# One more up projection by seven block products, and an even rate of wide pieces, in a two-layer decoder trunk

## The chip, the cores and the metric

The kernel runs on one core of a Trainium2 chip. The metric is the device time of one execution in microseconds (us); the time of the kernel before is the median of three runs.

## What is computed

Two post-norm residual layers on x, 256 tokens by 2048 channels, all in float32. Each layer has a mixer (layer 0: forgetting attention and block-sparse attention, layer 1: multi-head latent attention) and a SwiGLU feed-forward network. The change touches the feed-forward network alone:

```
for layer in range(DEPTH):                       # 2 layers
    y = mixer(x)
    x = layer_norm(alpha * x + y, ...)
    y = (silu(x @ w_gate) * (x @ w_up)) @ w_down  # 2048 -> 5632 -> 2048
    x = layer_norm(alpha * x + y, ...)
```

## The kernel before

**The work of TensorE** is a list of visits, written by `add_chunk` and `kmajor` and run in order by the loop at the end. A chunk is 512 output columns of one weight matrix; a visit takes 256 of its rows (a piece). float32 is had from three products of a high and a low part (`mm3`, lines 117 to 119): x high by w high, x high by w low, x low by w high.

**A plain piece** is 12 matmuls of 512 columns (two row blocks, two token tiles, three products). Its weights come by DMA into a `raw` tile, ScalarE copies them to the high part `wh` (line 425), VectorE subtracts to the low part `wl` (line 427).

**A wide piece** (`c.S`) does the same piece of a chunk by seven block products in place of eight (Winograd's form of Strassen's scheme): 21 matmuls of 256 columns into four PSUM banks A, B, C and D (`emit_s`, lines 453 to 455). Its weights need seven blocks, of which three are differences: VectorE makes these with three instructions (lines 383, 385, 386), ScalarE copies 1792 columns to `sh` (line 389), VectorE subtracts to `sl` (line 392). That last pair is owed and is paid behind the next piece's split (`owe`, `pay`). When a wide chunk is done, `drain_s` combines the four banks: one copy on ScalarE and five instructions on VectorE (lines 484 to 489). For an up chunk the product with the gate follows in one instruction (line 1093); a plain up has two (line 1089).

**The activations' blocks** for the wide pieces, `XS`, are made by `xs_batch` at the start of each feed-forward network, in four batches beside up 0 (VectorE lines 901 to 914).

**Order.** The network has 11 column groups f of 512. `ffn_part` first lists the plain visits: up f, and after f = 1, 3, 5, 7 and 10 the down projection of the groups so far (`down`). Gates 2 to 10 and the ups in `UPS` are wide; their pieces, in the order gate 2, gate 3, and so on, with an up of `UPS` right behind its gate, are mixed into the plain visits at a rate per plain visit k, `want`:

```
        for k, v in enumerate(flat):
            visits.append(v)
            want = max(want + (0 if k < 9 else 0.575 if k < 62 else 0.74 if k < 132 else 0.9),
                       ns + 1 if k in near else 0)
            while ns < min(len(gates), int(want)):
```

The product of gate and up is transposed on TensorE (`h_T`, line 602, four transposes a token tile) behind visits that `after_up` names: for a plain up, the first plain visit (f odd) or the second (f even) after its last piece; for a wide up, the first plain visit that begins a chunk. `ptile("tp")` puts the transposes into the pair of PSUM banks that the plain chunk before had, so they wait for VectorE twice: for the product (line 1089 or 1093) and for the reading of those banks (line 930 or 932 for a down chunk, which adds the result to the residual).

**Buffers.** Four pairs `wh`, `wl` serve plain pieces, two pairs `sh`, `sl` wide ones, while wide pieces are near; splits are made in the order of the pieces.

Of the kernel before, what the change touches and what calls it, by code (L numbers as in the profile page):

```python
# [53 lines left out]
def trunk_kernel(ctx: ExitStack, tc: tile.TileContext, x, ab_w_in, b_f, ab_w_out,  # L54
# [70 lines left out]
    def add_chunk(name, xs, kslots, srcs, tags=None):  # L125
        subs = []
        o = 0
        for n in srcs[0]:
            subs.append((n, o))
            o += n  # L130
        c = Chunk(name, xs, kslots, subs, srcs[1], tags or ("mm",) * len(subs))
        c.n = o
        chunks[name] = c
        return c

    def kmajor(c, hs=None):
        for h in (range(c.nh) if hs is None else hs):
            visits.append((c, h, (0, 1)))
# [18 lines left out]
    def lead_begin(c):  # L157
        for t in (0, 1):
            for h in range(LEAD):
                visits.append((c, h, (t,)))  # L160
        kmajor(c, range(LEAD, c.nh))

    def rows(w, k0, cols):
        return [(o, n, w[k0:k0 + 256, c0:c0 + n].rearrange("(k p) c -> p k c", p=P))
                for o, n, c0 in cols]
# [31 lines left out]

    GROUPS = ((0, 1), (2, 3), (4, 5), (6, 7), (8, 9, 10))
    NF = 11
    UPS = (4, 8)  # L200
    PLAIN = (0, 1)
    h_done = set()
    after_up = {}
# [2 lines left out]
    def ffn_part(layer):  # L206
        def wide(nm, w, f):
            return add_chunk(f"{nm}{layer}_{f}", "X", K16, ([512], lambda h: rows(
                w[layer], h * 256, [(0, 512, f * 512)])))

        def down(gi):
            grp = GROUPS[gi]
            slots = [4 * (f % 4) + k for f in grp for k in range(4)]
            for n in range(4):
                c = add_chunk(f"d{layer}_{gi}_{n}", "Y", slots, (
                    [512], lambda h, n=n: rows(
                        w_down[layer], grp[0] * 512 + h * 256, [(0, 512, n * 512)])))
                if gi == len(GROUPS) - 1 and n == 3:
                    (lead_final if layer == 1 else lead_end)(c)
                else:  # L220
                    kmajor(c)

        g0 = wide("g", w_gate, 0)
        g0.pair = 0
        lead_begin(g0)
        base = len(visits)
        for f in range(NF):
            if f == 1:
                kmajor(wide("g", w_gate, 1))
            c = wide("u", w_up, f)  # L230
            if f in UPS:
                c.S = True
            else:
                kmajor(c)
            if f in (1, 3, 5, 7):
                down(f // 2)
        down(len(GROUPS) - 1)
        flat = visits[base:]
        del visits[base:]
        ends = {}  # L240
        for f in range(NF):
            if f not in UPS:
                e = ends[f] = max(k for k, v in enumerate(flat) if v[0].name == f"u{layer}_{f}")
                o = e + 2 - f % 2
                after_up[layer, f] = [(v[0].name, v[1], v[2]) for v in flat[o:o + 3]]
        gates = []
        for f in range(len(PLAIN), NF):
            c = wide("g", w_gate, f)
            c.S = True
            gates += [(c, h, (0, 1)) for h in range(8)]  # L250
            if f in UPS:
                gates += [(chunks[f"u{layer}_{f}"], h, (0, 1)) for h in range(8)]
        near = {ends[f] + 2 for f in (1, 3, 5, 7, 9)}
        ns, want = 0, 0.0
        for k, v in enumerate(flat):
            visits.append(v)
            want = max(want + (0 if k < 9 else 0.575 if k < 62 else 0.74 if k < 132 else 0.9),
                       ns + 1 if k in near else 0)
            while ns < min(len(gates), int(want)):
                visits.append(gates[ns])  # L260
                ns += 1
                c = gates[ns - 1][0]
                f = int(c.name[3:])
                if ns % 8 == 0 and c.name[0] == "g" and f not in UPS:
                    assert k < ends[f] - 1, (k, ns, ends)
        assert ns == len(gates)
        for f in UPS:
            e = max(k for k, v in enumerate(visits) if v[0].name == f"u{layer}_{f}")
            rest = [v for v in visits[e + 1:] if not v[0].S]
            o = next(k for k, v in enumerate(rest) if v[1] == 0)  # L270
            after_up[layer, f] = [(v[0].name, v[1], v[2]) for v in rest[o:o + 2]]

    w_out_part("oa", ab_w_out[0])
    ffn_part(0)
    wi = mla_w_in[0]
    c = add_chunk("m0", "X", K16, ([512], lambda h: rows(wi, h * 256, [(0, 512, 0)])))
# [8 lines left out]
    for nm in order:  # L285
# [8 lines left out]
        kmajor(c)  # L294
    w_out_part("om", mla_w_out[0])
    ffn_part(1)


# [1163 lines left out]
```

## Time and profile before

| | |
|---|---|
| median of 3 runs (lowest, highest) | 2145.41 us (2145.27, 2146.47) |
| profiled execution, its own time | 2146.55 us |
| its span | 2144.7 us |
| granted TensorE clock, mean | 0.998 |
| TensorE / VectorE / ScalarE busy | 99% / 78% / 50% |
| HBM read | 402.56 MB, 190 GB/s over the span |

The span is that of the profiled execution; 1.9 us lie around it. Matmuls are pipelined and their ends are modelled, so a busy share of 99% does not show the gaps between matmuls; those are read from start times. The two feed-forward networks lie at about 436 to 1145 us and 1432 to 2144 us of the span.

### The profile page before, as it was taken

To read this page: it belongs to the slowest core of one execution; us is meant where nothing else is said; L and a number is where in the kernel's file an instruction comes from. 1 tells how busy PE (TensorE), PEld (TensorE's weight loads), DVE (VectorE), ACT (ScalarE), POOL (GpSimd) and SP (SyncE) were. 2 spreads that over 40 slices of the span, in tenths; PEclk is the share of its full clock that TensorE was granted. 3 is DMA by queue.
4 is the path that set the end of the run, shared out by engine and by line. 5 is a ranking of instruction groups with operands and counts; after the bars stand their busy time and mean duration, and the time that the engine had idled before them with its cause. 6 is when DMAs were issued, how large, how long until landed. Compare 5 with 4: busy or idle time off the path is not lost.

```text
span 2144.7 us, 31708 instructions
## 1 busy us (share of the span) xinstructions
PE 2120.4 (99%) x12570; PEld 1864.7 (87%) x12570; DVE 1674.0 (78%) x2173; ACT 1061.6 (50%) x1212; POOL 94.5 (4%) x142
## 2 busy tenths in 40 slices
PE   9999999999999999999999999999999999999998
PEld 9899998788888888888888999878888888888886
DVE  5555656798888998899866676688888989889875
ACT  5444544355545555555534665445444555555551
POOL 2100000100000000000001331010000000000000
PEclk9999999999999999999999999999999999999999
DMA  8565555556555556555865533745555556555582
GB/s 287 176 204 165 172 184 199 198 174 207 195 191 190 189 190 203 187 187 184 295 193 164 176 129 137 284 139 182 188 189 192 180 190 203 187 190 199 184 293 77
DMA packets 230341, 410.41 MB, mean 191 GB/s; under 512 B 14089, under 2 KB 58161, under 8 KB 229169
## 3 DMA queue, kind: packets, MB, share of 16 engines
q1 hardware_dynamic: 230192, 408.40, 57.3%
q8 instruction: 98, 1.61, 0.3%
q14 instruction: 51, 0.41, 0.1%
HBM read 402.56 MB, written 5.78 MB: 190 GB/s over the span
## 4 chain that ended last, share of the span: by engine, by line
PE 58%; issue 35%; DVE 5%; ACT 1%; POOL 1%; DMA 0%; SPq 0%; DVEq 0%; ACTq 0%; POOLq 0%
PE mm L117 11%; PE mm L118 11%; PE mm L119 11%; PE mm L512 3%; PE mm L516 3%; PE mm L514 3%; PE tp L602 2%; PE att L118 1%; PE att L119 1%; PE att L117 1%; PE sA L454 1%; PE sB L454 1%; PE sC L454 1%; PE sC L455 1%; PE sB L453 1%
## 5 line engine op out<-in xcount | busy, mean ns | idle before, releaser
L425 ACT ACTIVATE wh<-raw 128x1024 fp32r<-128x1024 f32 (+3 forms) x403 | 417.5, 1040 | 416.2 <-PE mm L119 161.9
L427 DVE TENSOR_TENSOR wl<-raw,wh 128x1024 fp32r<-128x1024 f32 (+3 forms) x403 | 482.3, 1206 | 133.1 <-ACT wh L425 131.9
L392 DVE TENSOR_TENSOR sl<-sraw,sh 128x1792 fp32r<-128x1792 f32 x176 | 356.2, 2024 | 64.6 <-ACT sh L389 63.9
L389 ACT ACTIVATE sh<-sraw 128x1792 fp32r<-128x1792 f32 x176 | 298.9, 1698 | 145.1 <-DVE sraw L386 141.9
L117 PE MATMUL mm<-wh,XH 128*128 128x512 f32 (+3 forms) x820 | 319.9, 390 | 0.0
L118 PE MATMUL mm<-wl,XH 128*128 128x512 f32 (+3 forms) x820 | 316.8, 386 | 0.0
L119 PE MATMUL mm<-wh,XL 128*128 128x512 f32 (+3 forms) x820 | 316.3, 386 | 0.0
L117 PE MATMUL mm<-wh,YH 128*128 128x512 f32 (+1 forms) x768 | 303.9, 396 | 0.0
L118 PE MATMUL mm<-wl,YH 128*128 128x512 f32 (+1 forms) x768 | 302.9, 394 | 0.0
L119 PE MATMUL mm<-wh,YL 128*128 128x512 f32 (+1 forms) x768 | 302.4, 394 | 0.0
L119 PEld LDWEIGHTS mm<-wh,XL 128*128 128x128 f32 x820 | 153.9, 188 | 33.2
L117 PEld LDWEIGHTS mm<-wh,XH 128*128 128x128 f32 x820 | 154.4, 188 | 28.0
L118 PEld LDWEIGHTS mm<-wl,XH 128*128 128x128 f32 x820 | 154.1, 188 | 27.7
L119 PEld LDWEIGHTS mm<-wh,YL 128*128 128x128 f32 x768 | 144.1, 188 | 34.6
L117 PEld LDWEIGHTS mm<-wh,YH 128*128 128x128 f32 x768 | 144.5, 188 | 29.6
L118 PEld LDWEIGHTS mm<-wl,YH 128*128 128x128 f32 x768 | 144.2, 188 | 29.5
L383 DVE TENSOR_TENSOR sraw<-sraw 128x512 f32<-128x512 f32 x176 | 120.5, 685 | 0.0
L512 PE MATMUL mm<-XH,wh 128*128 128x256 f32 x364 | 104.3, 286 | 0.0
L514 PE MATMUL mm<-XH,wl 128*128 128x256 f32 x364 | 102.6, 282 | 0.0
L516 PE MATMUL mm<-XL,wh 128*128 128x256 f32 x364 | 102.5, 282 | 0.0
L453 PE MATMUL sA<-sh,XH 128*128 128x256 f32 x352 | 100.9, 287 | 0.0
L454 PE MATMUL sA<-sl,XH 128*128 128x256 f32 x352 | 98.8, 281 | 0.5 <-DVE sl L392 0.4
(302 smaller groups left out, 4447.6 us busy)
## 6 DMA issues: line engine op xcount, KB each, us to landing
raw<-in_ffn_w_down_dram SPq DMA_DIRECT2D x160, 512.0 KB, 5.2
sraw<-in_ffn_w_gate_dram SPq DMA_DIRECT2D x149, 512.0 KB, 3.9
raw<-in_ffn_w_up_dram SPq DMA_DIRECT2D x137, 512.0 KB, 4.7
raw<-in_ab_w_in_dram SPq DMA_DIRECT2D x80, 256.0 KB, 3.1
sraw<-in_ffn_w_up_dram SPq DMA_DIRECT2D x39, 512.0 KB, 3.9
raw<-in_ffn_w_gate_dram SPq DMA_DIRECT2D x27, 512.0 KB, 4.6
sraw<-in_ab_w_in_dram SPq DMA_DIRECT2D x48, 256.0 KB, 3.3
raw<-in_ab_w_out_dram SPq DMA_DIRECT2D x22, 512.0 KB, 3.6
```

The source lines that it names most:

```text
L117: nc.tensor.matmul(o, lh, rh, start=start, stop=False)
L118: nc.tensor.matmul(o, lh, rl, start=False, stop=False)
L119: nc.tensor.matmul(o, ll, rh, start=False, stop=stop)
L389: nc.scalar.activation(sh, r[:, 256:2048], AF.Copy)
L392: nc.vector.tensor_tensor(sl, r[:, 256:2048], sh.bitcast(F32), op=ALU.subtract)
L425: nc.scalar.activation(wh[:, a:b], r[:, a:b], AF.Copy)
L427: nc.vector.tensor_tensor(wl[:, a:b], r[:, a:b], wh[:, a:b].bitcast(F32), op=ALU.subtract)
L453: nc.tensor.matmul(o, h, w[0][:, q], start=first, stop=False)
L454: nc.tensor.matmul(o, h, w[1][:, q], start=False, stop=False)
L512: nc.tensor.matmul(o, wh[:, kk, a:a + P], XH[:, slot, :], start=first, stop=False)
L514: nc.tensor.matmul(o, wl[:, kk, a:a + P], XH[:, slot, :], start=False, stop=False)
L516: nc.tensor.matmul(o, wh[:, kk, a:a + P], XL[:, slot, :], start=False, stop=last)
```

## The change

`UPS` becomes (2, 4, 8): the eight pieces of up 2 are wide in both layers, where they were plain. The rate is 0 for the first seven plain visits and 0.77 per plain visit after them, in place of 0 for nine, 0.575 to visit 61, 0.74 to visit 131 and 0.9 from there.

```diff
-    UPS = (4, 8)
+    UPS = (2, 4, 8)
...
-            want = max(want + (0 if k < 9 else 0.575 if k < 62 else 0.74 if k < 132 else 0.9),
+            want = max(want + (0 if k < 7 else 0.77),
                        ns + 1 if k in near else 0)
```

Layer 0's list had 173 plain and 88 wide visits behind gate 0, and has 165 and 96 now (layer 1's has seven more plain visits, at its very end). The wide ones ended behind plain visit 138, and end behind 130; the plain visits after that are as many as before. The order moves on all engines; three places on VectorE matter below. In the rows, `raw` and `sraw` are loaded weights, `wl`, `sl` low parts, `xt` and `gt` the tiles of up and of gate, `X` the residual.

**Up 0's end, layer 0.** Before, from the split of the piece ahead of gate 2's first:

```order
L427 TENSOR_TENSOR wl_95<-raw_91,wh_94 128x1024
L914 TENSOR_TENSOR XS_4150<-gt_3530,XS_4149 128x1024
L383 TENSOR_TENSOR sraw_93<-sraw_93 128x512
L385 TENSOR_TENSOR sraw_93<-sraw_93 128x256
L386 TENSOR_TENSOR sraw_93<-sraw_93 128x256
L1089 TENSOR_TENSOR gt_3529<-gt_3529,mm_4131 128x512
L1089 TENSOR_TENSOR gt_3529<-gt_3529,mm_4132 128x512
L427 TENSOR_TENSOR wl_97<-raw_88,wh_96 128x1024
L392 TENSOR_TENSOR sl_103<-sraw_93,sh_102 128x1792
```

Now, from the blocks of gate 2's second piece:

```order
L383 TENSOR_TENSOR sraw_93<-sraw_93 128x512
L385 TENSOR_TENSOR sraw_93<-sraw_93 128x256
L386 TENSOR_TENSOR sraw_93<-sraw_93 128x256
L901 TENSOR_TENSOR xt_3526<-XH,XL 128x1024
L392 TENSOR_TENSOR sl_103<-sraw_93,sh_102 128x1792
L906 TENSOR_TENSOR gt_3530<-xt_3526 128x2x128
L907 TENSOR_TENSOR gt_3530<-gt_3530,xt_3526 128x2x128
L908 TENSOR_TENSOR gt_3530<-xt_3526 128x2x128
L909 TENSOR_TENSOR gt_3530<-xt_3526,gt_3530 128x2x128
L427 TENSOR_TENSOR wl_97<-raw_88,wh_96 128x1024
L914 TENSOR_TENSOR XS_4146<-gt_3530,XS_4145 128x1024
L1089 TENSOR_TENSOR gt_3529<-gt_3529,mm_4127 128x512
```

Between the first batch of `XS` and up 0's product (line 1089), layer 0 had the blocks of one wide piece and no `sl`; now it has the blocks and the `sl` of two. Layer 1 had the blocks and the `sl` of one and three whole batches; now it has two of each and the fourth batch's line 914 too. On TensorE the first wide piece now stands ahead of the plain visit behind which up 0 is transposed.

**Up 4's end, layer 0.** Before, with the reading of the last down chunk's banks (line 932) first:

```order
L932 TENSOR_TENSOR X_3525<-X_3525,mm_5982 128x512
L932 TENSOR_TENSOR X_3525<-X_3525,mm_5983 128x512
L392 TENSOR_TENSOR sl_103<-sraw_93,sh_102 128x1792
L484 TENSOR_TENSOR xt_3526<-xt_3526,sD_5721 128x256
L485 TENSOR_TENSOR xt_3526<-xt_3526,sA_5720 128x256
L486 TENSOR_TENSOR xt_3526<-xt_3526,sB_5722 128x2x256
L488 TENSOR_TENSOR xt_3526<-xt_3526,sB_5722 128x256
L489 TENSOR_TENSOR xt_3526<-xt_3526,sC_5723 128x2x256
L1093 TENSOR_TENSOR gt_3529<-gt_3529,xt_3526 128x1024
```

Now:

```order
L484 TENSOR_TENSOR xt_3526<-xt_3526,sD_5913 128x256
L485 TENSOR_TENSOR xt_3526<-xt_3526,sA_5912 128x256
L486 TENSOR_TENSOR xt_3526<-xt_3526,sB_5914 128x2x256
L488 TENSOR_TENSOR xt_3526<-xt_3526,sB_5914 128x256
L489 TENSOR_TENSOR xt_3526<-xt_3526,sC_5915 128x2x256
L1093 TENSOR_TENSOR gt_3529<-gt_3529,xt_3526 128x1024
L383 TENSOR_TENSOR sraw_93<-sraw_93 128x512
L385 TENSOR_TENSOR sraw_93<-sraw_93 128x256
L386 TENSOR_TENSOR sraw_93<-sraw_93 128x256
L427 TENSOR_TENSOR wl_97<-raw_88,wh_96 128x1024
L932 TENSOR_TENSOR X_3525<-X_3525,mm_6146 128x512
L932 TENSOR_TENSOR X_3525<-X_3525,mm_6147 128x512
```

The reading of the banks moved from ahead of the drain to behind it and behind a split. On TensorE, one plain visit stood between up 4's last piece and its transposes, and two stand there now. Up 8 had three plain visits and a wide one there, and has two plain ones now, in the same order as up 4.

**Up 2's end, layer 0, now** (it was plain before):

```order
L930 SCALAR_TENSOR_TENSOR X_3525<-X_3525,mm_4918 128x512
L930 SCALAR_TENSOR_TENSOR X_3525<-X_3525,mm_4919 128x512
L392 TENSOR_TENSOR sl_105<-sraw_92,sh_104 128x1792
L484 TENSOR_TENSOR xt_3526<-xt_3526,sD_4703 128x256
L485 TENSOR_TENSOR xt_3526<-xt_3526,sA_4702 128x256
L486 TENSOR_TENSOR xt_3526<-xt_3526,sB_4704 128x2x256
L488 TENSOR_TENSOR xt_3526<-xt_3526,sB_4704 128x256
L489 TENSOR_TENSOR xt_3526<-xt_3526,sC_4705 128x2x256
L1093 TENSOR_TENSOR gt_3529<-gt_3529,xt_3526 128x1024
```

This is the order that up 4 had before, with one plain visit between the last piece and the transposes.

## Rows read from the trace of the kernel before

**Rows 1.** The page, its span and its part 1.

```profile
span 2144.7 us, 31708 instructions
...
PE 2120.4 (99%) x12570; PEld 1864.7 (87%) x12570; DVE 1674.0 (78%) x2173; ACT 1061.6 (50%) x1212; POOL 94.5 (4%) x142
```

**Rows 2.** Timeline of TensorE: start us, us, engine, line, operation [idle before].

```profile
1008.87 0.28 PE L453 MATMUL sA<-sh,XH 128*128 128x256 f32 x1
...
1011.36 0.39 PE L117 MATMUL mm<-wh,XH 128*128 128x512 f32 x1
...
1014.14 0.40 PE L117 MATMUL mm<-wh,XH 128*128 128x512 f32 x1
```

**Rows 3.** Busy time by stretch, layer 0: PE, PEld, DVE, ACT, POOL, clock, DMA.

```profile
467.00:691.00 224.00, 223.30 (x1285) 194.41 (x1284) 190.96 (x217) 113.57 (x99) 0.00 (x0) 1.00 0.58 195
691.00:1016.00 325.00, 323.21 (x1936) 284.65 (x1935) 294.65 (x343) 167.17 (x141) 0.00 (x0) 1.00 0.57 190
```

**Rows 4.** Waits of VectorE, 467 to 691 us: total us, times, longest.

```profile
DVE wl L427 <- ACT wh L425: 16.4, 17, 1.8
DVE sl L392 <- ACT sh L389: 11.5, 25, 1.0
```

**Rows 5.** Waits of VectorE, 691 to 1016 us.

```profile
DVE sl L392 <- ACT sh L389: 18.2, 31, 0.9
DVE wl L427 <- ACT wh L425: 3.0, 6, 0.6
```

**Rows 6.** Timeline of TensorE, layer 0: the first transposes after ups 0, 1, 4, 8.

```profile
463.88 0.60 PE L602 MATMUL tp<-ident,gt 128*128 128x128 f32 x4
...
527.41 0.66 PE L602 MATMUL tp<-ident,gt 128*128 128x128 f32 x4 [0.70 <-DVE gt L1089]
...
701.18 0.40 PE L119 MATMUL mm<-wh,YL 128*128 128x512 f32 x1
702.93 0.66 PE L602 MATMUL tp<-ident,gt 128*128 128x128 f32 x4 [1.35 <-DVE gt L1093]
...
965.30 0.66 PE L602 MATMUL tp<-ident,gt 128*128 128x128 f32 x4 [0.22 <-DVE X L932]
```

**Rows 7.** The same, layer 1: ups 0, 1, 4, 8.

```profile
1460.19 0.65 PE L602 MATMUL tp<-ident,gt 128*128 128x128 f32 x4 [0.50 <-DVE gt L1089]
...
1524.35 0.65 PE L602 MATMUL tp<-ident,gt 128*128 128x128 f32 x4 [1.30 <-DVE gt L1089]
...
1699.86 0.66 PE L602 MATMUL tp<-ident,gt 128*128 128x128 f32 x4 [1.34 <-DVE gt L1093]
...
1962.84 0.66 PE L602 MATMUL tp<-ident,gt 128*128 128x128 f32 x4 [0.81 <-DVE X L932]
```

**Rows 8.** Timeline of VectorE: up 0's products, layer 0 and layer 1.

```profile
463.01 1.28 DVE L1089 TENSOR_TENSOR gt<-gt,mm 128x512 f32<-128x512 f32 x2
...
1458.86 1.28 DVE L1089 TENSOR_TENSOR gt<-gt,mm 128x512 f32<-128x512 f32 x2
```

**Rows 9.** Timeline of VectorE, layer 0, around up 4's end.

```profile
698.89 0.42 DVE L484 TENSOR_TENSOR xt<-xt,sD 128x256 f32<-128x256 f32 x1
...
701.65 1.22 DVE L1093 TENSOR_TENSOR gt<-gt,xt 128x1024 f32<-128x1024 f32 x1
702.79 0.68 DVE L383 TENSOR_TENSOR sraw<-sraw 128x512 f32<-128x512 f32 x1
...
704.31 1.22 DVE L427 TENSOR_TENSOR wl<-raw,wh 128x1024 fp32r<-128x1024 f32 x1
705.44 0.68 DVE L114 TENSOR_TENSOR YL<-tp,YH 128x512 fp32r<-128x512 f32 x1
```

**Rows 10.** Timeline of VectorE, layer 0, around up 8's end.

```profile
953.28 2.03 DVE L392 TENSOR_TENSOR sl<-sraw,sh 128x1792 fp32r<-128x1792 f32 x1 [0.77 <-ACT sh L389]
955.22 0.41 DVE L484 TENSOR_TENSOR xt<-xt,sD 128x256 f32<-128x256 f32 x1
...
964.57 1.28 DVE L932 TENSOR_TENSOR X<-X,mm 128x512 f32<-128x512 f32 x2
```

## The prediction, made before the change was run

> **What bounds the kernel.** I read the page first: TensorE is busy for 99% of the span, VectorE for 78% [rows 1]. The first figure hides small gaps, since ends are modelled; so I took start times next. A wide piece takes 1011.36 - 1008.87 = 2.49 us on TensorE, a plain one 14.14 - 11.36 = 2.78 us [rows 2]. The list of visits, at these prices, is what sets the time: the order leaves TensorE few waits. Then the busy time by stretch, for whoever might be late: at a rate of 0.575 wide pieces VectorE is busy 191.0 of 224 us (85%), at 0.74 it is 294.7 of 325 us (91%), with TensorE at its full clock of 2.4 GHz in both [rows 3]. What the rest of VectorE's time is, its waits say. A wait of `wl` for ScalarE's `wh` mostly means that VectorE is ahead and has no free buffer: 16.4 us at 0.575 [rows 4], only 3.0 us at 0.74 [rows 5]. The wait of `sl` for `sh` (18.2 us in 31 waits there) is the latency of the wide split itself and gives nothing back. So at 0.74 VectorE's chain fills some 99% of the time (3.0 of 325 us are left); at 0.575 it had 7% to spare. Last, the transposes of the product, where TensorE waits for VectorE by name [rows 6, 7]. The bracket counts from a modelled end: from 701.18 to 702.93 is 1.75 us where 0.23 is usual, so 1.52 us are lost against a bracket of 1.35. I add 0.17 to each bracket: 0.87, 1.52 and 0.39 us in layer 0 (ups 1, 4, 8), 0.67, 1.47, 1.51 and 0.98 us in layer 1 (ups 0, 1, 4, 8), 7.4 us in all.
>
> **The change, term by term.** A difference of 0.2%, 4.3 us, is about what a measurement of this kernel can tell from none.
>
> *The products.* 16 pieces (8 in each layer) go from 2.78 to 2.49 us: -16 x 0.29 = **-4.6 us**. All of it lies on TensorE's path, since TensorE has work at every moment there. Bytes and DMA issues stay the same, a wide piece is the same 512 KB; SP's and POOL's queues get nothing new.
>
> A rule of the Trainium skill speaks against this term. The page "TensorE: Matmul & The Clock Gate", section "Back-to-back issue gap", says that in a stream of weight loads and matmuls both set the spacing, about 81 ns at 128 columns and 131 ns at 512; halfway, as an estimate, 98 ns at 256 columns, so that 21 short matmuls would cost 2.06 us against 1.57 us for 12 long ones and the term would be +7.8 us. The trace disagrees: 2.49 / 21 = 119 ns against 2.78 / 12 = 232 ns [rows 2].
>
> *VectorE's work.* The price of a wide split is its blocks, 704.31 - 702.79 = 1.52 us [rows 9], and its `sl`, 955.22 - 953.28 = 1.94 us [rows 10]; a plain split is 705.44 - 704.31 = 1.13 us [rows 9]. Where VectorE is ahead, this is covered. I go through the places where TensorE waits for it.
>
> *Up 0.* The first wide piece comes two plain visits earlier, into the stretch in which VectorE makes `XS`. In layer 0 the product's first half ended at 463.01 + 0.68 = 463.69 [rows 8], 0.2 us ahead of the transposes at 463.88, which did not wait [rows 6]. By the order, VectorE now has 1.52 + 2 x 1.94 = 5.4 us more ahead of that product, and TensorE one wide piece, 2.49 us: a stall of up to 5.4 - 2.5 - 0.2 = 2.7 us. Short waits that VectorE has there can take part of it; none to all, I take 2.0. In layer 1 it gets 1.52 + 1.94 + 1.13 (line 914, priced as the split of the same size) = 4.6 us more; 4.6 - 2.5 + 0.67 = 2.8, I take 2.4, which is 1.7 over the old stall. Together **+3.7 us** (0 to 4.8).
>
> *Up 1.* Its transposes stood one plain visit behind its last piece; now a wide visit of 2.49 us comes between, more than either stall. The 0.87 and 1.47 us go: **-2.3 us** (0 if VectorE is late by as much).
>
> *Up 2.* It was plain and had no stall. Now it has the order that up 4 had, with one plain visit (2.78 us) to hide the drain and the product, which took from 698.89 to 702.87 [rows 9]. That cost 1.52 us at up 4, so **+3.0 us** in two layers (2 to 5).
>
> *Ups 4 and 8.* Both now have two plain visits, 5.56 us, but the banks for the transposes are read by line 932 behind the drain. From the end of the up's last piece: before, at up 4 this was 701.18 + 0.23 - 2.78 = 698.63, and the drain began 0.26 later. Drain and product take 702.79 - 698.89 = 3.90 us, the next blocks 1.52, a plain split 1.13, the first half of line 932 0.68: 7.5 us, a stall of 1.9 us. At up 8 the drain began 1.14 us behind that end (955.22 against 964.91 less three plain visits and a wide one), because `sl` waited for `sh` [rows 10]; with that it is 2.8 us. In layer 1 the transposes wait for the second half, 0.6 us more, as the stalls of up 8 show (0.39 and 0.98). I take 2.3 and 2.9 us: 10.4 us for four, less the 4.4 us they cost before: **+6.0 us** (4.4 to 9).
>
> *The rest.* Transposes of plain ups 3, 5, 7 and 9 keep a wide visit ahead of them and had no stall. The tail behind the wide pieces has the same plain visits as before. ScalarE, half idle, does 8 longer copies a layer and is waited for only through VectorE; I cost it at nothing.
>
> Sum: -4.6 + 3.7 - 2.3 + 3.0 + 6.0 = +5.8 us, so 2152.3 from the profiled execution's 2146.55 us. Its own time lies 1.1 us above the median of the runs; from that, 2151.2 us.
>
> A check from VectorE's side. A layer adds 8 x (1.52 + 1.94) = 27.7 us of wide splits, 8 x 0.35 = 2.8 us of waits for `sh` (18.2 us [rows 5] over the 52 wide pieces that 325 us hold at 0.74), 3.90 - 1.28 = 2.6 us for up 2's drain and product in place of its two plain products, and drops 8 x 1.13 = 9.0 us: 24 us. It had 16.4 + 3.0 = 19.4 us in which it was ahead [rows 4, 5]. If all of that can be used it falls behind by 4.7 us a layer, +9 us in all. So **VectorE becomes the bound of the stretch**, and the two ways of counting agree within 4 us. The stalls above are counted at their places, so I keep to them and add 0.8 us for short waits for `sl`: **2152.0 us**.
>
> **The rivals.**
>
> *VectorE keeps ahead (faster).* If short waits inside VectorE's order close up and the order at ups 0, 2, 4 and 8 costs no more than before, what is left is -4.6 - 2.3: 2138.5 us. For it: the early stretch did have 16 us to spare. Against: line 1089 was only 0.2 us early in layer 0. It decides at whether VectorE begins the products within 0.3 us of their due time.
>
> *Ups 4 and 8 stay as they were (same).* If the banks are read in time, +6.0 goes: 2146.0 us with the small waits. For it: at up 8 line 932 stood behind the drain before too, and only 0.39 and 0.98 us were lost. Against: a plain visit and a wide one less stand there now to hide it.
>
> *VectorE's lead can't be used (slower by more).* If only three quarters of the 19.4 us are worth anything, it falls behind by 24 - 14.6 = 9 us a layer: 2163 us. For it: an even rate leaves it no stretch to recover in.
>
> *Weight loads set the spacing (slower).* Loads were busy for 1864.7 us in 12,570, 148 ns each [rows 1]; 21 of them would be 3.1 us, over a plain piece's 2.78: +5.3 in place of -4.6 us, 2162 us with the stalls. Against: rows 2 show 119 ns a matmul. This is the place of the skill's rule above, which the rows don't bear out.
>
> **How the numbers follow.** Forecast 0.50 (its own range 2147 to 2158), VectorE ahead 0.14, ups 4 and 8 as before 0.22, lead unusable 0.12, loads 0.02. Faster by over 0.2% (under 2141.1) is the first rival, 0.14. Same (to 2149.7) is the second, 0.22, and a quarter of the forecast, 0.12. Slower is the rest, 0.52. The range from 2143 to 2162 leaves out the first rival and a third of the case with the lead unusable (its own range is 2157 to 2169), and takes in the loads' 2162 us: 0.18.
>
> **What would show it.** In the changed profile: wide pieces still 2.49 us; transposes with a bracket of 1 to 3 us behind ups 0, 2, 4 and 8 in both layers, none behind up 1; those of ups 4 and 8 released by line 932; VectorE at 90% or more from 470 us on, with its waits for `wh` down to a few us a layer. I am wrong if ups 4 and 8 wait under 1 us, if the waits for `wh` stay above 10 us a layer, or if TensorE's longest waits stand at wide pieces, for `sl`, and not at transposes.

## The result and the profile after

The changed kernel takes **2176.05 us** (median of 4 runs, 2175.20 to 2178.81), the kernel before 2145.94 us beside it (4 runs, 2145.27 to 2146.80): a ratio of 1.0142, 95% interval 1.0125 to 1.0160. It is slower by 30 us. The forecast was 2152.0 us, with a range from 2143 to 2162: the sign was right, the size was not, and the range missed.

The page of the changed kernel, its span and its part 1 [rows 1 are those of before]; the profiled execution took 2178.81 us itself:

```profile
span 2176.7 us, 32083 instructions
PE 2128.8 (98%) x12714; PEld 1876.7 (86%) x12714; DVE 1712.9 (79%) x2229; ACT 1076.9 (49%) x1214; POOL 94.5 (4%) x142
```

The page hides the loss almost wholly: TensorE is busy 98% in place of 99%, and part of the 8.4 us that it gained in busy time is matmuls that ran slower. So I read the transposes by the timeline, as [rows 6, 7] were read. TensorE, the first transposes after ups 0, 2, 4 and 8 in layer 0, then the same in layer 1:

```profile
469.27 0.84 PE L602 MATMUL tp<-ident,gt 128*128 128x128 f32 x4 [2.69 <-DVE gt L1089]
...
564.98 0.65 PE L602 MATMUL tp<-ident,gt 128*128 128x128 f32 x4 [1.35 <-DVE gt L1093]
...
722.02 1.00 PE L602 MATMUL tp<-ident,gt 128*128 128x128 f32 x4 [3.65 <-DVE X L932]
...
976.04 0.66 PE L602 MATMUL tp<-ident,gt 128*128 128x128 f32 x4 [1.43 <-DVE X L932]
...
1478.71 0.66 PE L602 MATMUL tp<-ident,gt 128*128 128x128 f32 x4 [2.47 <-DVE gt L1089]
...
1575.72 1.12 PE L602 MATMUL tp<-ident,gt 128*128 128x128 f32 x4 [2.68 <-DVE gt L1093]
...
1736.71 1.12 PE L602 MATMUL tp<-ident,gt 128*128 128x128 f32 x4 [4.96 <-DVE X L932]
...
1992.19 0.66 PE L602 MATMUL tp<-ident,gt 128*128 128x128 f32 x4 [1.58 <-DVE X L932]
```

Each stands where the prediction put it, with the releaser it named, and up 1 has none. With 0.17 added to each bracket they make 22.2 us; 17.8 were forecast and 7.4 were there before. That is +14.8 us of the span's +32.0 (2176.7 less 2144.7).

**A term that the sum did not have** shows in the granted clock. Busy time by stretch of the changed kernel (columns as in [rows 3]; the clock is third from the end), behind up 0's transposes and behind up 4's:

```profile
469.60:473.00 3.40, 3.40 (x18) 3.40 (x17) 3.33 (x6) 1.50 (x1) 0.00 (x0) 0.50 0.00 0
473.00:476.40 3.40, 3.40 (x20) 2.91 (x20) 3.40 (x4) 1.64 (x3) 0.00 (x0) 1.00 0.02 5
...
722.20:725.60 3.40, 3.40 (x18) 3.40 (x18) 3.40 (x4) 2.49 (x3) 0.00 (x0) 0.50 0.02 3
```

For 3.4 us TensorE ran at 1.2 GHz in place of 2.4. There are five such stretches in the two networks, at 469.6, 722.2, 1479.9, 1575.5 and 1735.9 us (the last of 6.8 us). Each goes with one of the five brackets of 2.47 us or more: the last two begin 0.2 and 0.8 us before the wait ends, the others behind it; the three brackets of 1.35 to 1.58 us had none behind them. The networks of the kernel before had none but at the very end. TensorE's timeline in the longest, the first matmuls of one wide piece and of the plain piece after it:

```profile
1737.48 0.56 PE L453 MATMUL sA<-sh,XH 128*128 128x256 f32 x1
...
1742.11 0.63 PE L117 MATMUL mm<-wh,YH 128*128 128x512 f32 x1
```

The piece took 4.63 us, 2.49 is usual [rows 2]. By start times the five stretches cost 1.7, 1.8, 1.6, 1.7 and 3.0 us, **9.8 us** in all.

**A second one** is a group of waits at the third piece of a down chunk. Some come from ScalarE's queue, which I had costed at nothing. ScalarE's timeline, changed kernel, at the end of up 3 (columns as before, ACT is ScalarE):

```profile
662.06 0.38 ACT L483 ACTIVATE gt<-sA 128x256 f32<-128x256 f32 x1
667.28 1.06 ACT L1084 ACTIVATE gt<-gt 128x1024 f32<-128x1024 f32 x1 [4.83 <-DVE gt L489]
668.25 1.04 ACT L425 ACTIVATE wh<-raw 128x1024 fp32r<-128x1024 f32 x1
669.19 0.58 ACT L113 ACTIVATE YH<-tp 128x512 fp32r<-128x512 f32 x1
```

The Silu of a wide gate (line 1084) waits for the end of the drain on VectorE, and behind it, in the same queue, waits the copy of the transposed product to `YH`, which the down chunk needs. TensorE's timeline there:

```profile
669.82 0.51 PE L117 MATMUL mm<-wh,YH 128*128 128x512 f32 x1 [0.85 <-ACT YH L113]
...
671.20 0.50 PE L119 MATMUL mm<-wh,YL 128*128 128x512 f32 x1 [0.64 <-DVE YL L114]
```

By start times the waits at this place lost 6.7 us at ups 3 and 7 of both layers, and none before. Only 2.0 us of them are waits for ScalarE's `YH`, at up 3. Another 1.6 us are for `YL` (line 114) at up 3, just behind, and 3.0 us are for `YL` at up 7, where no Silu stands in the way. Up 7 in layer 0, VectorE and TensorE:

```profile
945.27 0.68 DVE L114 TENSOR_TENSOR YL<-tp,YH 128x512 fp32r<-128x512 f32 x1
```

```profile
946.01 0.51 PE L119 MATMUL mm<-wh,YL 128*128 128x512 f32 x1 [1.41 <-DVE YL L114]
```

VectorE came to line 114 without a wait of its own, straight from two plain splits and an `sl`, while `YH` had been done since 943.4 us: that is VectorE's lateness again. Waits of wide pieces for `sl` grew by another 3.5 us or so. With the products' -4.6: -4.6 + 14.8 + 9.8 + 6.7 + 3.5 = 30.2 of the 32.0 us.

**Why VectorE is late** I read from its own chain, from the first batch of `XS` (line 901) to the last `sl` (line 392). Before, this runs in layer 0 from 438.8 to 1050.5 us and in layer 1 from 1434.5 to 2047.5; after, from 435.5 to 1065.3 and from 1445.2 to 2081.4. Busy time in these stretches, first before, then after (DVE is the third figure behind the comma, without the counts):

```profile
438.80:1050.50 611.70, 609.18 (x3556) 532.33 (x3555) 544.10 (x632) 314.73 (x269) 0.00 (x0) 1.00 0.57 192
1434.50:2047.50 613.00, 608.81 (x3554) 532.03 (x3553) 544.28 (x632) 314.57 (x269) 0.00 (x0) 1.00 0.57 192
```

```profile
435.50:1065.30 629.80, 616.46 (x3649) 541.24 (x3648) 566.22 (x663) 324.79 (x274) 0.00 (x0) 0.99 0.57 190
1445.20:2081.40 636.20, 619.69 (x3649) 543.50 (x3648) 566.96 (x663) 324.70 (x274) 0.00 (x0) 0.99 0.56 188
```

And VectorE's waits in layer 0's stretch, before and after:

```profile
DVE sl L392 <- ACT sh L389: 31.9, 59, 1.0
DVE wl L427 <- ACT wh L425: 19.4, 23, 1.8
```

```profile
DVE sl L392 <- ACT sh L389: 45.4, 67, 3.0
DVE wl L427 <- ACT wh L425: 8.0, 13, 1.6
```

The chain grew by 18.1 us in layer 0 and 23.2 in layer 1. VectorE's idle time in it, the length less the busy time, was 67.6 and 68.7 us and is 63.6 and 69.2: all but 4 us of the added work in layer 0, and all of it in layer 1, came out as added length. VectorE's work grew by 22.1 and 22.7 us, as forecast (27.7 + 2.6 - 9.0 = 21.3). The wait for `sh` grew by 13.5 us, where 2.8 were forecast (in layer 1 it went from 32.0 to 47.3); the wait for `wh`, in which VectorE is ahead, gave back 11.4 of its 19.4 us (layer 1: 23.8 to 9.1). In layer 0 other, shorter waits gave back the remaining 6.1 us.

What the wait for `sh` is, VectorE's timeline shows. Before, at one wide piece in two plain ones:

```profile
615.43 1.23 DVE L427 TENSOR_TENSOR wl<-raw,wh 128x1024 fp32r<-128x1024 f32 x1 [1.82 <-ACT wh L425]
617.02 2.02 DVE L392 TENSOR_TENSOR sl<-sraw,sh 128x1792 fp32r<-128x1792 f32 x1 [0.36 <-ACT sh L389]
```

After, at one in one:

```profile
626.81 2.03 DVE L392 TENSOR_TENSOR sl<-sraw,sh 128x1792 fp32r<-128x1792 f32 x1 [0.78 <-ACT sh L389]
...
630.28 1.22 DVE L427 TENSOR_TENSOR wl<-raw,wh 128x1024 fp32r<-128x1024 f32 x1
632.27 2.03 DVE L392 TENSOR_TENSOR sl<-sraw,sh 128x1792 fp32r<-128x1792 f32 x1 [0.77 <-ACT sh L389]
```

Where one plain split alone stands between a wide piece's blocks and its `sl`, the wait for `sh` is about 0.4 us if VectorE had waited for `wh` in between, and 0.77 us if it runs through; with two plain splits in between the trace has a mean of 0.1 to 0.3 us. That was so before the change too ([rows 10] have 0.77). What changed is mostly the count: in each layer one split alone stood there at 34 of 88 wide pieces before, and stands there at 43 of 96 now. Of these, VectorE ran through at 27 and 25 before (layers 0 and 1) and at 40 and 40 now. Of the growth of 13.5 us in layer 0, some 7 us are nine more such places at 0.77, 1.5 us are places that lost their wait for `wh`, and most of the rest is two single waits of 2.5 and 3.0 us, in which ScalarE came late to the copy because it had waited for TensorE. A pair of a wide and a plain piece takes VectorE 632.27 - 626.81 = 5.46 us so, and TensorE 2.49 + 2.78 = 5.27. In an alternation VectorE can't catch up, and every drain, product and residual comes on top. (At a rate of 0.77 only some of the turns are such a pair.)

### The profile page after: what moved, and what is told of

Its sections match the earlier page's. It is cut to its first block, busy times and chain, and to the rows that moved or that the text cites. A ratio compares the mean times of both kernels' runs of the same rounds, so it can differ in the third digit from the quotient of the medians.

```text
span 2176.7 us, 32083 instructions
## 1 busy us (share of the span) xinstructions
PE 2128.8 (98%) x12714; PEld 1876.7 (86%) x12714; DVE 1712.9 (79%) x2229; ACT 1076.9 (49%) x1214; POOL 94.5 (4%) x142
## 4 chain that ended last, share of the span: by engine, by line
PE 50%; issue 35%; DVE 8%; ACT 3%; DMA 2%; POOL 1%; SPq 0%; ACTq 0%; DVEq 0%; POOLq 0%
PE mm L117 9%; PE mm L118 9%; PE mm L119 9%; PE mm L512 3%; PE mm L514 3%; PE mm L516 3%; DVE sl L392 3%; ACT sh L389 2%; DMA raw<-in_ffn_w_down_dram 2%; PE tp L602 1%; PE att L119 1%; PE att L118 1%; PE att L117 1%; DVE wl L427 1%; PE sA L454 1%
## 5 line engine op out<-in xcount | busy, mean ns | idle before, releaser
L425 ACT ACTIVATE wh<-raw 128x1024 fp32r<-128x1024 f32 (+4 forms) x393 | 408.0, 1043 | 369.6 <-DMA raw<-in_ffn_w_down_dram 132.5
L427 DVE TENSOR_TENSOR wl<-raw,wh 128x1024 fp32r<-128x1024 f32 (+4 forms) x393 | 470.1, 1207 | 102.6 <-ACT wh L425 98.1
L392 DVE TENSOR_TENSOR sl<-sraw,sh 128x1792 fp32r<-128x1792 f32 x192 | 388.6, 2024 | 93.0 <-ACT sh L389 92.7
L389 ACT ACTIVATE sh<-sraw 128x1792 fp32r<-128x1792 f32 x192 | 326.4, 1700 | 228.8 <-DVE sraw L386 201.6
L117 PE MATMUL mm<-wh,XH 128*128 128x512 f32 (+3 forms) x768 | 299.1, 389 | 0.0
L118 PE MATMUL mm<-wl,XH 128*128 128x512 f32 (+3 forms) x768 | 296.3, 386 | 0.0
L119 PE MATMUL mm<-wh,XL 128*128 128x512 f32 (+3 forms) x768 | 295.7, 385 | 0.0
L383 DVE TENSOR_TENSOR sraw<-sraw 128x512 f32<-128x512 f32 x192 | 131.4, 684 | 0.1
L453 PE MATMUL sB<-sh,XS 128*128 128x256 f32 x384 | 108.9, 284 | 0.0
L454 PE MATMUL sB<-sl,XS 128*128 128x256 f32 x384 | 108.8, 283 | 0.0
L455 PE MATMUL sB<-sh,XS 128*128 128x256 f32 x384 | 108.6, 283 | 0.0
```

Source lines behind the costliest of these rows:

```text
L117: nc.tensor.matmul(o, lh, rh, start=start, stop=False)
L118: nc.tensor.matmul(o, lh, rl, start=False, stop=False)
L119: nc.tensor.matmul(o, ll, rh, start=False, stop=stop)
L383: nc.vector.tensor_tensor(v[:, 4:6], v[:, 0:1].broadcast_to([P, 2, 256]), v[:, 1:3], op=ALU.subtract)
L389: nc.scalar.activation(sh, r[:, 256:2048], AF.Copy)
L392: nc.vector.tensor_tensor(sl, r[:, 256:2048], sh.bitcast(F32), op=ALU.subtract)
```

## The experiments

In the expectations, P is the theory that the change's order costs the time at single places (transposes that stand too early), T that VectorE's work for wide pieces is more than the stretch can hold, so that lateness moves from place to place; C is the half clock, S the Silu in ScalarE's queue, L the latency of `sh`. The kernel before ran beside each group of runs, at medians of 2146.1 to 2146.6 us.

### Later transposes (e2, e3)

e2: the transposes of ups 2, 4 and 8 one plain chunk later. e3: those of up 0 two visits later as well.

```diff
-            o = next(k for k, v in enumerate(rest) if v[1] == 0)
+            o = [k for k, v in enumerate(rest) if v[1] == 0][1]
```

```diff
-                o = e + 2 - f % 2
+                o = e + (4 if f == 0 else 2 - f % 2)
```

> The change, with the transposes of ups 2, 4 and 8 moved one chunk later (behind the second plain visit that begins a chunk after the up's last piece; before: the first). Theory P (places): the loss sits where TensorE waits for VectorE in front of these transposes, 1.5 + 3.8 + 1.6 us in layer 0 and 2.8 + 5.1 + 1.7 us in layer 1 (16.6 us), and in the half-clock stretches that follow up 4 in both layers and up 2 in layer 1 (about 6.3 us). Both go: 2176 - 23 = about 2153 us. Theory T (throughput): VectorE has too little time in the whole stretch, so TensorE waits elsewhere instead (for sl at wide pieces, for up 0): 2168 us or more.

> The same, and up 0's transposes moved two plain visits later. Theory P: up 0's waits of 2.9 and 2.6 us and the half-clock stretch behind each (1.6 us) go too, another 8.7 us: about 2144 us, a little faster than before the change. Theory T: the work left undone shows as waits for sl in the first 100 us of each network: 2160 us or more.

Measured: e2 2170.23 us (ratio 1.0110, interval 1.0095 to 1.0125), e3 2169.38 us (1.0106, 1.0091 to 1.0122). TensorE's waits in e3, layer 0 (columns as in [rows 4]):

```profile
PE sA L454 <- DVE sl L392: 6.9, 8, 2.0
...
PE tp L602 <- DVE X L930: 1.3, 1, 1.3
...
PE tp L602 <- DVE X L932: 0.5, 1, 0.5
```

The brackets at transposes make 20.8 us in the changed kernel and 4.3 here (1.8 in layer 0, 2.5 in layer 1), but the time fell by 6 to 7. By start times TensorE now lost 9.7 and 9.4 us at wide pieces, for `sl` (3.7 and 4.2 in the changed kernel), and two half-clock stretches were still there, where P expected none. P falls; the lateness moved, as T has it.

### No idle time ahead of the transposes (e4)

Eight products with a tile of zeros stand ahead of the first transposes of ups 0, 2 and 4. They add zero to an accumulating bank; the waits stay as long, but TensorE works in part of them.

```diff
+    zero = const.tile([P, P], F32R, name="zero")
+    nc.gpsimd.tensor_scalar(zero, ident, 0.0, None, op0=ALU.mult)
...
+                if t == 0 and f in (0, 2, 4):
+                    o_ = visits[cur[0]][0].ps[0][0]
+                    for _ in range(8):
+                        nc.tensor.matmul(o_, zero, XH[:, 0:2, :], start=False, stop=False)
```

> The change, with eight products of a zero tile of 512 columns (1.9 us) put on TensorE in front of the first transposes of ups 0, 2 and 4; they add zero to an accumulation that is running, and the waits stay. Theory C (clock): the half-clock stretches come from TensorE standing idle there, and cost about 9.5 us in all; with 1.9 us of each wait filled they vanish: about 2167 us, granted clock back from 0.993 to 0.998. Rival: the waits alone are the cost and the low clock comes from elsewhere or costs nothing: 2176 us or a little more, clock as in the change.

Measured: 2169.02 us (1.0103, 1.0088 to 1.0119), 7.0 less than the change. Layer 0's up 4, TensorE:

```profile
718.01 2.03 PE L1104 MATMUL mm<-XH,zero 128*128 128x512 f32 x8
721.82 0.66 PE L604 MATMUL tp<-ident,gt 128*128 128x128 f32 x4 [1.78 <-DVE X L934]
```

The transposes begin at 721.82 us, 722.02 in the changed kernel: the stall is the same, but its transposes take 0.66 us, and one stretch of half clock is left of five, behind up 4 of layer 1, where a wait of 2.12 us was left behind the zero products. C holds: some 7 us are the clock's alone.

### The Silu of wide gates two visits later (e5)

```diff
+    slow = []
...
-                    nc.scalar.activation(g_, g_, AF.Silu)
+                    slow.append((cur[0] + 2, lambda: nc.scalar.activation(g_, g_, AF.Silu)))
...
+        while slow and slow[0][0] <= i:
+            slow.pop(0)[1]()
```

> The change, with the Silu of each wide gate put two visits later into ScalarE's queue. Theory S: TensorE's waits at the third piece of a down chunk (YH, YL; 1.0 + 0.8 + 1.6 us in layer 0, 1.0 + 0.8 + 1.5 us in layer 1) come from that Silu, which stands in ScalarE's queue waiting for VectorE's drain, ahead of the copies of the transposed product: they go, about 2169.5 us. Rival: the copies are late because VectorE is late, whatever stands in ScalarE's queue: 2175 us or more.

Measured: 2169.75 us (1.0110, 1.0093 to 1.0127). The size is that of S. The waits for `YH` are gone, but those for `YL` stayed, at some 2.4 to 2.7 us a layer; so most of the gain of 6.3 us came in another way. By start times, the waits of wide pieces for `sl` fell by some 4 us in the two layers together, and four stretches of half clock are left of five, the one behind up 2 of layer 1 gone. S has the mechanism for the 2.0 us of `YH`, and the size of its forecast is luck.

### All three edits, on the change and on the kernel before (e6, e7)

The edits of e3 and e5 together, once on the changed kernel and once on the kernel before.

> The change with the three moves together: ups 2, 4, 8 and up 0 transposed later, the Silu of a wide gate two visits later. By now theory T says that VectorE's own chain sets the feed-forward stretch: from its first batch of XS to its last sl it takes 627 to 637 us in the change and in every run so far, and moving TensorE's waits does not shorten it. T: that chain stays at about 625 us and the time at 2163 to 2167 us. Theory P (the places alone): 2176 - 23 - 9 - 6 = about 2138 us.

> The kernel before with the three edits that gave the changed kernel 17 us back together: transposes of ups 4 and 8 one chunk later, those of up 0 two visits later, Silu of wide gates two visits later. Before loses 7.4 us at transposes and about as much at other places. If the three edits are improvements of any order: 2139 to 2143 us. If they only mend what the changed order breaks (theory T, VectorE's lateness moves from place to place): 2144 to 2148 us.

Measured: e6 2158.61 us (1.0059, 1.0044 to 1.0074); e7 2142.16 us (0.9975, 0.9967 to 0.9984). e7 is faster than the kernel before by a quarter of a per cent, as the expectation had it for edits that help any order; T had said 2144 to 2148 us. With the same edits on both sides the change still costs 16 us, so the three edits, and the clock with them, take off a little under half of its 30 us. The expectation for e6 by T (2163 to 2167 us) was too high, that by P (2138) far too low. VectorE's chain in e6 is 624.1 and 620.9 us long (T expected about 625), and in e7 609.9 and 609.1.

### Less VectorE work for the same number of products (e8)

e8 leaves out the last two of a wide piece's seven blocks, on VectorE and in ScalarE's copy, and multiplies another block in their place. TensorE has as many products as in the change, but they are no longer those of the two layers.

```diff
-        nc.vector.tensor_tensor(v[:, 6], v[:, 1], v[:, 5], op=ALU.subtract)
-        nc.vector.tensor_tensor(v[:, 7], v[:, 3], v[:, 6], op=ALU.subtract)
...
-            nc.scalar.activation(sh, r[:, 256:2048], AF.Copy)
+            nc.scalar.activation(sh[:, 0:1280], r[:, 256:1536], AF.Copy)
...
-            nc.vector.tensor_tensor(sl, r[:, 256:2048], sh.bitcast(F32), op=ALU.subtract)
+            nc.vector.tensor_tensor(sl[:, 0:1280], r[:, 256:1536], sh[:, 0:1280].bitcast(F32), op=ALU.subtract)
...
+        q = min(q, 4)
```

> The change with work taken from VectorE and ScalarE and nothing else: the last two of a wide piece's seven blocks are not made and not split (two block instructions less, sl and sh of 1280 in place of 1792 columns); TensorE runs the same 21 products with other blocks. About 1.3 us less on VectorE per wide piece, 129 us a layer. T: VectorE is far ahead, the stretch is TensorE's: the waits of before (9 us) and the half-clock stretches go and the 4.6 us of the products show: about 2133 to 2138 us. If loads, buffers or the order on TensorE set the stretch: over 2160 us.

Measured: 2137.20 us (0.9957, 0.9940 to 0.9973), 39 less than the change, with its order, its places and its number of wide pieces untouched. VectorE's waits, layer 0:

```profile
DVE wl L425 <- ACT wh L423: 62.0, 58, 1.9
DVE sl L390 <- ACT sh L387: 48.7, 51, 4.1
```

VectorE is ahead for 62 us where it was for 8, though its wait for `sh` is as long as after. T holds in this: with less work on VectorE (and a shorter copy on ScalarE) the loss is gone, though order and places are the change's. What the products are worth then this run doesn't tell: it is 9 us under the kernel before, but no run takes the same work from that kernel.

### 88 wide pieces with the change's evenness (e17)

```diff
-    UPS = (2, 4, 8)
+    UPS = (2, 6)
...
-            want = max(want + (0 if k < 7 else 0.77),
+            want = max(want + (0 if k < 7 else 0.69),
```

> The changed kernel with ups 2 and 6 wide in place of 2, 4 and 8, and an even rate of 0.69: 88 wide pieces a layer as before, with up 2 wide, an even rate and the early first wide piece, as in the change. Theory T (the number of wide pieces is what VectorE can't carry): VectorE's balance is that of before, so 2146 to 2155 us; the half clock and the stall behind up 2 may stay. Rival (the even rate or up 2's place costs the time, not the number): 2162 us or more.

Measured: 2152.65 us (1.0026, 1.0017 to 1.0035). VectorE's waits, layer 0:

```profile
DVE sl L392 <- ACT sh L389: 35.1, 56, 2.7
DVE wl L427 <- ACT wh L425: 19.8, 26, 2.1
```

As many wide pieces as before, and VectorE is ahead as long as before. Up 2 by blocks, the even rate and the early first piece cost 6 us together; the 8 pieces more in each layer go with the other 24. The comparison isn't clean: e17 also has up 6 wide in place of 4 and 8, and a rate of 0.69 in place of 0.77, so the 24 us can't be put down to the number of pieces alone.

### 512 columns of `sl` on GpSimd (e13, e14)

```diff
-            nc.vector.tensor_tensor(sl, r[:, 256:2048], sh.bitcast(F32), op=ALU.subtract)
+            nc.gpsimd.tensor_tensor(sl[:, 1280:1792], r[:, 1536:2048], sh[:, 1280:1792].bitcast(F32),
+                                    op=ALU.subtract)
+            nc.vector.tensor_tensor(sl[:, 0:1280], r[:, 256:1536], sh[:, 0:1280].bitcast(F32),
+                                    op=ALU.subtract)
```

> The changed kernel, with the last 512 of the 1792 columns of every wide piece's low part (sl) subtracted by GpSimd instead of VectorE. VectorE's 1.94 us become about 1.39, 0.55 us less for each of 96 pieces, 53 us a layer, where VectorE's chain was 18 to 23 us a layer too long; GpSimd has rows of 1.5 to 1.6 us for 128x512, beside VectorE's 1.39. Theory T (VectorE's chain with wide pieces is the bound): 2133 to 2150 us, TensorE's lost time under 14 us a layer, VectorE's waits of wl for wh above 20 us a layer. Rival (the load is not the bound, the places of the transposes and ScalarE's queue are): 2165 us or more. A third outcome, VectorE itself slowed beside GpSimd: sl's instruction stays above 1.7 us, and the time stays near 2170.

> The kernel before, with the same 512 columns of sl moved to GpSimd. VectorE was not the bound there: T expects 2140 to 2147 us, no more than its 8.6 and 10.1 us of lost TensorE time a layer could give. If the changed kernel with GpSimd is faster than this one by 2 us or more, the seven-block products of up 2 pay off once VectorE has room.

Measured: on the change 2226.18 us (1.0372, 1.0358 to 1.0386), on the kernel before 2177.53 us (1.0144, 1.0130 to 1.0158). Timeline of e13, GpSimd (POOL) and VectorE:

```profile
597.84 2.60 POOL L392 TENSOR_TENSOR sl<-sraw,sh 128x512 fp32r<-128x512 f32 x1 [6.09 <-ACT sh L389]
599.21 1.79 DVE L383 TENSOR_TENSOR sraw<-sraw 128x512 f32<-128x512 f32 x1
...
603.89 1.49 DVE L394 TENSOR_TENSOR sl<-sraw,sh 128x1280 fp32r<-128x1280 f32 x1 [0.77 <-ACT sh L389]
603.93 2.61 POOL L392 TENSOR_TENSOR sl<-sraw,sh 128x512 fp32r<-128x512 f32 x1 [3.49 <-ACT sh L389]
```

`sl` did get shorter here, 1.49 us for 2.02; over the stretch from 470 to 1050 us its mean is 1.86 us, and that of line 383 is 1.19 (mean ns is the second figure behind the bar):

```profile
L394 DVE TENSOR_TENSOR sl<-sraw,sh 128x1280 fp32r<-128x1280 f32 x87 | 161.9, 1861 | 33.3 <-ACT sh L389 32.7
...
L383 DVE TENSOR_TENSOR sraw<-sraw 128x512 f32<-128x512 f32 x87 | 103.4, 1189 | 0.8 <-DMA sraw<-in_ffn_w_gate_dram 0.7
```

In the timeline the next block instruction (line 383), 0.68 us by itself [rows 9], took 1.79: begun at 599.21, it ended 0.56 us after GpSimd's subtraction did (at 600.44). The two engines work one after the other. The Trainium skill, page "SBUF — State Buffer", section "SBUF: two separate sides", says that the two share one pair of ports, and that where VectorE's instruction has two inputs in SBUF, whichever of the two engines begins first holds the pair for its whole instruction while the other stands still; the trace agrees, 1.79 us against 0.68. So this run made VectorE's chain longer, not shorter, and the time followed it up, by 50 us on the change and by 31 on the kernel before. The third outcome of the expectation came, with `sl` above 1.7 us in the mean, but far beyond its size: it said near 2170. T's ranges for both runs were missed, and neither run tests T, since VectorE got no room.

### The latency of `sh` (e9, e10, e18, e19, e20)

e9 and e10: ScalarE copies the three blocks that need no subtraction first, and the rest after; on the change and on the kernel before.

```diff
+        nc.scalar.activation(sh[:, 0:768], r[:, 256:1024], AF.Copy)
...
-            nc.scalar.activation(sh, r[:, 256:2048], AF.Copy)
+            nc.scalar.activation(sh[:, 768:1792], r[:, 1024:2048], AF.Copy)
```

> The change with ScalarE's copy of a wide piece in two: the three loaded blocks (768 columns) ahead of VectorE's blocks, the four made ones (1024 columns) behind. VectorE's own work is the same; its sl no longer has to wait 1.7 us for sh behind the blocks. T: these waits (46 us a layer, 32 before the change) fall below 15, VectorE's chain from 630 to about 600 us, and the stretch becomes TensorE's: about 2135 to 2142 us. Rival: only VectorE's busy time counts, or ScalarE's longer queue delays wh as much: 2165 us or more.

> The kernel before with the same two-part copy. T: VectorE had 1% to spare there and TensorE lost about 9 us to it; most of that goes: 2137 to 2141 us. Rival: no change, 2146 us.

Measured: e9 2170.42 us (1.0114, 1.0099 to 1.0129), e10 2146.99 us (1.0006, 0.9996 to 1.0015). What T expected (2135 to 2142 us of e9, 2137 to 2141 of e10) did not come; e10 came out as its rival said, unchanged. Waits of VectorE and of ScalarE in e9, layer 0:

```profile
DVE wl L428 <- ACT wh L426: 44.0, 36, 3.3
...
DVE sl L393 <- ACT sh L390: 2.1, 4, 1.3
```

```profile
ACT sh L382 <- PE sC L456: 123.2, 59, 5.0
```

The wait for `sh` went from 45.4 to 2.1 us, and the wait for `wh` from 8.0 to 44.0. The first copy now stands in ScalarE's queue until TensorE has freed its buffer, and the plain pieces' `wh` wait behind it.

e18, e19 and e20 cover the latency in another way: the owed pair is paid up to two visits later, so that the next wide piece's blocks come before `sl`. e18 is the change with it, e19 the change with the edits of e6 too, e20 the kernel of e7 with it.

```diff
-        if any(cur[0] - o["at"] >= 1 for o in owed):
+        if any(cur[0] - o["at"] >= 2 for o in owed):
```

> The changed kernel, with the owed pair of a wide piece (ScalarE's copy to sh, VectorE's sl) paid up to two visits later in place of one: where a wide piece follows a plain one, VectorE makes the next wide piece's blocks (1.52 us) before it subtracts sl, and the copy's latency is covered. Theory L: the wait of 0.77 us that VectorE has for sh whenever it is not ahead (41 and 45 waits of over 0.6 us in a layer, against 27 and 26 before) is the term that the sum took at 0.35; without most of it VectorE's chain is 15 to 25 us a layer shorter: 2145 to 2160 us, waits of sl for sh under 25 us a layer. Rival: the piece buffer, now held longer, makes the blocks wait for their DMA and the transposes wait as long: 2168 us or more, with waits of the blocks for sraw's DMA above 10 us a layer.

> The same with the later transposes of ups 0, 2, 4 and 8 and the later Silu. By L: 2138 to 2150 us. By the rival: 2155 us or more.

> The kernel before with the later transposes, the later Silu and the later pair. VectorE is not the bound there, so by L no more than its remaining 7 us a layer of lost TensorE time is to be had: 2137 to 2142 us, within 2 us of the kernel before with the first two alone (2142.16 us). If the pair's later place costs waits of its own: 2145 us or more.

Measured: e18 2225.49 us (1.0363, 1.0348 to 1.0378), e19 2210.53 us (1.0306, 1.0288 to 1.0325), e20 2182.36 us (1.0168, 1.0154 to 1.0183). VectorE's waits in e18, layer 0:

```profile
DVE wl L427 <- ACT wh L425: 28.8, 35, 2.2
DVE sraw L383 <- DMA sraw<-in_ffn_w_gate_dram: 20.2, 20, 2.2
DVE sl L392 <- ACT sh L389: 17.0, 30, 1.2
DVE sraw L383 <- DMA sraw<-in_ffn_w_up_dram: 7.0, 7, 1.9
```

The wait for `sh` fell to 17.0 us, as L had it, but the rival came: 27.2 us of waits for the pieces' DMA, which starts when a piece buffer comes free, and the plain pieces' `wh` late behind it. So with two buffers for loaded wide pieces neither of the two ways covered the latency without paying elsewhere. A third buffer was not tried. e20 shows the same cost on the kernel of e7: 40 us more, where L expected it within 2 us.

## Why the prediction was wrong, point by point

- **The products, -4.6 us: right in price.** A wide piece still takes 2.49 us at full clock, so TensorE has 4.6 us less work. That this comes out as time once VectorE has room no run shows by itself; e8 (2137.2 us) is in keeping with it.
- **Up 1, -2.3 us: right.** Its stalls are gone.
- **Up 0, +3.7; up 2, +3.0; ups 4 and 8, +6.0 us: right in place and releaser, small in size.** Up 0 stalled for 2.86 and 2.64 us (2.0 and 2.4 forecast), up 2 for 1.52 and 2.85 (1.5), ups 4 and 8 for 3.82, 1.60, 5.13 and 1.75, 12.3 us (10.4): 4.4 us more in all. Up 4 was the worse of the last two, not up 8.
- **The failed step is the check from VectorE's side, by which the sum was taken for whole**: "2.8 us of waits for `sh`" and "16.4 + 3.0 = 19.4 us in which it was ahead. If all of that can be used". The work in it was right to 1.4 us. The lead could not be used: the waits for `wh` did fall by 11.4 and 14.7 us, but the waits for `sh` rose by 13.5 and 15.3, and VectorE's idle time as a whole went from 67.6 to 63.6 and from 68.7 to 69.2 us. So the chain is 18 and 23 us longer, not 4.7. The wait for `sh` was priced at 0.35 us, the mean over all kinds of turns; a piece with one plain split behind its blocks has 0.77, and nine more in each layer are of that kind. The rest of the rise is places that lost their wait for `wh`, and single long waits. The two ways of counting agreed within 4 us because both were short.
- **ScalarE "at nothing"** failed: 2.0 us of waits for `YH` behind the Silu in its queue. I had looked at ScalarE's busy share (50%), not at what stands behind a wait. The other 4.7 us at the same pieces are waits for VectorE's `YL`, for which the sum had no term either; they stayed in e5.
- **The clock** had no term: 9.8 us, the largest one missing, of which e4 gave 7 back. I had priced a stall of 2.7 us as 2.7.
- **"Short waits for `sl`", +0.8 us**: 3.5. Together 4.4 + 6.7 + 9.8 + 2.7 = 23.6 us, which is the miss of 24.
- **The rivals.** "VectorE's lead can't be used" was the right one, with a price too small (2163 us): it took a quarter of the lead for unusable and left out that the wait for `sh` grows. Weight loads did not set the spacing.
- **The signs.** None of the three signs of being wrong showed: ups 4 and 8 waited for over 1 us, the waits for `wh` fell below 10 us a layer, and the longest waits stood at transposes. They asked where TensorE waits and not how long VectorE's chain is, so they could not catch this miss.

What stays open: how the 24 us that e17 leaves divide between VectorE's busy time, the latency of `sh`, and the order. e9 and e18 took the latency away and each put another wait in its place.

## What to carry to other kernels

Before adding work to an engine that is 90% busy in its stretch, work out its period for each kind of turn in the pattern, with the latency waits of that kind when it is not ahead, and count the turns: a one-in-one turn took VectorE 5.46 us against TensorE's 5.27, where the mean wait of 0.35 would have made it some 5.0. Idle time of which the releaser is another engine's answer to one's own last instruction was not spare here; the attempts to fill it with a split copy, a later pair or GpSimd moved it to a buffer, a DMA or a port. A stall is worth more than its length if TensorE's clock falls behind it, and keeping TensorE at work in it gives that part back.

## What the runs showed of the hardware

- At the end of a wait of TensorE of 2.5 to 5 us or just behind it, in networks otherwise at 2.4 GHz, the granted clock of the changed kernel was 0.5 for 3.4 us (6.8 once), which cost 1.6 to 1.8 us (3.0). With some 2 us of zero products in the wait (e4) it was not at four of the five places. The length of the wait alone doesn't settle it: in e2 such a stretch began 1.4 us behind a wait of 1.82 us.
- In e13, GpSimd's and VectorE's subtractions of two tiles ran one after the other: 1.79 us for an instruction of 0.68, and 1.19 us in the mean of 87.
